# Recurrent channels laid out by heads: gathers replaced by operands in place, two vector steps moved to accumulating DMAs

## The chip, the cores and the metric

The kernel runs on one core of a Trainium2 chip. Its engines are TensorE (PE, matrix multiplications; the profile calls its weight loads PEld), VectorE (DVE), ScalarE (ACT), GpSimd (POOL) and SyncE (SP). Each engine works off its own list of instructions in order; SP and POOL issue the DMAs. The metric is the device time of one execution in microseconds (us). The time before is 1534.15 us, the median of three runs (1534.04 to 1534.54).

## The reference

One layer of a decoder trunk over 1024 positions with 1024 channels: a projection to 7168 channels, a convolution branch and a recurrent branch of 1536 channels in 16 heads of 96, both gated and merged, an output projection, and an MLP. What matters here is the projection and the recurrent branch:

```python
h = rms_norm(x, g_mix[l])
z = jnp.einsum("bsd,de->bse", h, w_in[l]) + b_in[l]
va, ga, xb, gb, sa, sb = jnp.split(z, cuts, axis=-1)

u = va * jax.nn.sigmoid(ga)
u = causal_depthwise_conv(u, conv_a_w[l], conv_a_b[l])      # 31 taps
u = jax.nn.silu(layer_norm(u, ln_g[l], ln_b[l]))
...
v = causal_depthwise_conv(xb, conv_b_w[l], conv_b_b[l])     # 4 taps
v = rg_lru(v, w_rg_a[l], b_rg_a[l], w_rg_x[l], b_rg_x[l], lam[l])
...
def rg_lru(x, w_a, b_a, w_x, b_x, lam):
    r = jax.nn.sigmoid(block_diag_linear(x, w_a, b_a))      # per head, 96x96
    i = jax.nn.sigmoid(block_diag_linear(x, w_x, b_x))
    log_a = -LRU_C * r * jax.nn.softplus(-lam)
    a = jnp.exp(log_a)
    bterm = jnp.sqrt(-jnp.expm1(2.0 * log_a)) * i * x
    ...                                                     # h = a*h + bterm along the positions
```

All inputs and outputs are float32. The kernel multiplies float32 in three passes: every operand is split in a high part (rounded to the format fp32r) and a low part (the rest), and high x high, low x high and high x low are summed in PSUM.

## The kernel before

Channels stand on the 128 partitions and the 1024 positions on the free axis. A tile `T` is 128x1024 float32 (512 KB); there are 37 buffers of that size, and a tile waits for the last reader of the buffer that it gets.

The projection's first part runs over 28 chunks of 128 output channels, in the order `CH`: value and gate chunks of the convolution branch (VA, GA) and the twelve chunks of the recurrent branch (XB). A chunk is 24 pairs of operands by two halves of 512 positions, 48 matmuls, on line 726. The first three chunks are done before the loop; the loop over slots `s` = 3 to 27 does one chunk in each slot and, beside it, the work of chunks and heads that came before. The order of every engine's instructions is written out by hand (`manual_schedule`): the Python code is the order. Only DVE's is planned: `later` puts work on a list with a time when its input should be ready, `vector_work` works off that list by these times, and `fill` puts taps of the 31-tap convolution (`conv`) in between as long as a running estimate of DVE's clock stays below the next ready time. The estimates are fixed numbers; nothing on the chip feeds back into them.

**A weight chunk** is loaded by SP (`w_load`, two slots ahead) and split by `split_dma` (lines 63 to 67): ACT writes l = -w, a POOL DMA adds w to it in place (an accumulating DMA), ACT writes h = w in fp32r. So l is the low part, rounded by h's conversion.

**A tile of v**: `xb_out` evacuates chunk XB+t in the slot behind it: ACT writes xb and the last tap of v, DVE adds the other three taps (`rest`, line 486). `xb_parts` (line 492) then splits v: ACT writes vth, DVE subtracts to get vtl (line 462 is the one place from which `dve` calls its functions, so many DVE instructions bear that line).

**A head** has 96 channels, so head n of group g (four heads in three tiles) lies in one or two tiles of v. `head_load` (line 505) gathers its 96 rows of vth and vtl from the tiles into vh and vl by SP DMAs, by the table `PIECES`. `head_w` loads the two 96x96 gate weights, `head_w_parts` splits them. `head_mm(n, gi)` does the six matmuls of gate gi (lines 534 to 536) into the tag "ps2", of which there is one PSUM buffer. `head_gate` writes the sigmoid on ACT (line 542) and scatters its rows back to the tiles `gate[gi, t]` by SP DMAs (line 549).

In slot `s`, with `before` the head whose first gate's matmuls ran in the slot before, and `new` the head of this slot, the order on PE is: 36 matmuls of the chunk, `head_mm(before, 1)`, 12 matmuls, `head_mm(new, 0)`. On ACT: gate 0 of `before`, the evacuation of the chunk before, the split of the next weights, `scan_root`, `xb_parts`, gate 1 of `before`, the split of the next head's weights, `scan_exp`.

**The scan** of group g: in the slot behind the group's last head (`EXP`), `scan_exp` computes a and a tanh on ACT (six instructions of 128x1024, lines 558 and 559, behind a load of ACT's table), and `scan_in` multiplies gate 1 with v on DVE for tiles 3g and 3g+1, a slot later for 3g+2. `scan_root` takes square roots a slot later, `scan_tile` runs the scan (lines 575 to 578) in the slots behind. Slots 9, 14, 19 and 24 are the EXP slots.

**The convolution** (`conv`) ends by writing its tile to DRAM (`yd`) and adding it to the tile `ysum` on DVE (line 651), for the mean of the layer norm. Four of the eight convolutions end in the slots of the projection's first part, the others in the next stage.

**The next stage** (z) does the remaining 28 chunks in pairs by a scheme of 7 products of half size. The weights of the products are sums of blocks (`z_sums`, names zs) on DVE, then split by `z_lhs` (names zo), mostly with `split_dma` again. The inputs' sums xs and their parts are made in slots 23 to 27 (`XS`, `x_load`, `x_sum`, `x_parts`).

Of the kernel before, what the change touches and what calls it, by code (L numbers as in the profile page):

```python
# [9 lines left out]
F32 = mybir.dt.float32  # L10
# [3 lines left out]
ALU = mybir.AluOpType  # L14
# [16 lines left out]
def trunk_kernel(ctx: ExitStack, tc: tile.TileContext, x, xt_in, xt_eo, vecs, w_in, w_a_out, w_b_pl, w_b_sq,  # L31
# [12 lines left out]
    def T(name, dt=F32, shape=(P, S)):  # L44
        return tp.tile(list(shape), dt, tag="T", name=name)
# [77 lines left out]
    def H(name, tag, dt=F32):  # L123
        return qp.tile([HD, S], dt, tag=tag, name=name, bufs=4 if tag == "p" else 2)
# [310 lines left out]
    def at(e, cost, ready=0.0):  # L435
        clk[e] = max(clk[e], ready) + cost
        return clk[e] + 0.1
# [3 lines left out]
    def fill(until):  # L441
        while clk["V"] + 0.67 <= until:
            if taps["now"] is None:
                if taps["next"] is None:
                    if not taps["wait"] or taps["hold"]:
                        return taps["more"](until)
                    taps["next"] = conv(taps["wait"].pop(0))
                    next(taps["next"])
                taps["now"], taps["next"], taps["left"] = taps["next"], None, 48
            if next(taps["now"], None) is None:  # L450
                taps["now"] = None
                continue
            taps["left"] -= 1
            if taps["left"] == 4 and taps["wait"] and not taps["hold"]:

                taps["next"] = conv(taps["wait"].pop(0))
                next(taps["next"])

    def dve(cost, ready, f, *a):
# [2 lines left out]
        f(*a)  # L462
        return at("V", cost, ready)


    PIECES = [[(0, 0, 96, 0)], [(0, 96, 128, 0), (1, 0, 64, 32)],
              [(1, 64, 128, 0), (2, 0, 32, 64)], [(2, 32, 128, 0)]]

    vt = {}

# [20 lines left out]

    def xb_parts(t):
        vp_[t] = T(f"vth{t}", F32R), T(f"vtl{t}", F32R)
        nc.scalar.activation(vp_[t][0], vt[t], AF.Copy)
        h = vp_[t][0].bitcast(F32)
        later(at("A", 1.06), 1.22, nc.vector.tensor_tensor, vp_[t][1], vt[t], h, ALU.subtract)


    gws = {}
# [2 lines left out]
    gate = {}  # L502
    hd = dp.tile([12, P, S], F32, name="hd")

    def head_load(n):

        g, hh = divmod(n, 4)
        parts[n] = H(f"vh{n}", "p", F32R), H(f"vl{n}", "p", F32R)
        for (ti, p0, p1, d0) in PIECES[hh]:
            for a, b in zip(parts[n], vp_[3 * g + ti]):  # L510
                nc.sync.dma_start(a[d0:d0 + p1 - p0, :].bitcast(F32), b[p0:p1, :].bitcast(F32))

    def head_w(n):
        raw = rp.tile([HD, 2, HD], F32, tag="rraw", name=f"rraw{n}")
# [11 lines left out]
    gps = {}  # L526

    def head_mm(n, gi):
        vh, vl = parts[n]
        gh, gl = gws[n]  # L530
        gps[n, gi] = ps = PS(f"rg{n}_{gi}", "ps2")
        for hf, hs in enumerate(HALVES):
            o = ps[:HD, hs]
            nc.tensor.matmul(o, gh[:, gi, :], vh[:, hs], start=True, stop=False)  # L534
            nc.tensor.matmul(o, gl[:, gi, :], vh[:, hs], start=False, stop=False)
            nc.tensor.matmul(o, gh[:, gi, :], vl[:, hs], start=False, stop=True)  # L536
        at("P", 6 * MM)

    def head_gate(n, gi, ready):
        g, hh = divmod(n, 4)  # L540
        a = H(f"g{n}_{gi}", "g")
        nc.scalar.activation(a, gps.pop((n, gi))[:HD, :], AF.Sigmoid,  # L542
                             bias=(ba_c, bx_c)[gi][:, n:n + 1])
        at("A", 1.11, ready)
        for (ti, p0, p1, d0) in PIECES[hh]:
            t = 3 * g + ti
            if (gi, t) not in gate:
                gate[gi, t] = T(f"g{gi}_{t}")
            nc.sync.dma_start(gate[gi, t][p0:p1, :], a[d0:d0 + p1 - p0, :])

    at_, rooted = {}, {}

# [49 lines left out]
    def conv(j):  # L602
        u = ut.pop(j)
        acc, tmp = T(f"y{j}"), T(f"yt{j}")
        xe, xo = (u[:, h] for h in HALVES)
        p0, p2 = (acc[:, h] for h in HALVES)
        xs, p1 = (tmp[:, h] for h in HALVES)
        bias = cab_c[:, j:j + 1]

        def tap(d):  # L610
            w = WA - 1 - d
            return caw[:, w * 8 + j:w * 8 + j + 1]

        def tapsum(k):

            return tap(2 * k) if k == NE - 1 else csum[:, NE - 2 - k, j:j + 1]

        sub, add = ALU.subtract, ALU.add
        nc.scalar.activation(p0, xe, AF.Identity, scale=tap(0), bias=bias)
        nc.scalar.activation(p1, xo, AF.Copy, scale=tap(1))  # L620
        begun = at("A", 1.24)
        yield True

        def step(cost=0.67):
            at("V", cost)
            return True

        nc.vector.tensor_tensor(xs, xe, xo, add)
        yield step()
        nc.vector.tensor_scalar(p2, xs, tapsum(0), cab2[:, j:j + 1], ALU.mult, add)  # L630
        clk["V"] = max(clk["V"], begun)
        yield step(0.45)
        for k in range(1, NE):
            for o, a, c in ((p0, xe, tap(2 * k)), (p2, xs, tapsum(k)),
                            (p1, xo, tap(2 * k + 1) if k < NE - 1 else None)):
                if c is not None:
                    nc.vector.scalar_tensor_tensor(o[:, k:], a[:, 0:HS - k], c, o[:, k:],  # L637
                                                   ALU.mult, add)
                    yield step()
        nc.vector.tensor_tensor(p2, p2, p0, sub)  # L640
        yield step()
        nc.vector.tensor_tensor(p2, p2, p1, sub)
        yield step()
        nc.vector.tensor_tensor(p0[:, 1:], p0[:, 1:], p1[:, 0:HS - 1], add)
        nc.sync.dma_start(yd[j], acc)
        yield step()
        if j == 0:
            ysum.append(T("ysum"))
            nc.vector.tensor_copy(ysum[0], acc)
        else:  # L650
            nc.vector.tensor_tensor(ysum[0], ysum[0], acc, add)
        yield step(1.22)

# [40 lines left out]
    def later(ready, cost, f, *a):  # L696

        todo.append((ready, len(todo), cost, f, a))
# [9 lines left out]
    def w_load(s):  # L708
        if s < NC1:
            wraw[s] = load_w(w_in[CH[s]], f"win{s}")  # L710
# [77 lines left out]
    def z_get(n, f):  # L788
# [1 line left out]

    ENGINES = {mybir.EngineType.Activation, mybir.EngineType.DVE, mybir.EngineType.PE,
               mybir.EngineType.SP, mybir.EngineType.Pool}
    HS0 = [5 + 5 * (n // 4) + n % 4 for n in range(NH)]
    head_at = {s: n for n, s in enumerate(HS0)}

    EXP = {head_slot: g for g, head_slot in enumerate(HS0[4 * g + 3] + 1 for g in range(4))}
    XS = {23: ((x_load, 0),), 24: ((x_sum, 0),), 25: ((x_load, 1), (x_parts, 0, 6)),
          26: ((x_sum, 1), (x_parts, 0, 7, 5)), 27: ((x_parts, 0, 4), (x_parts, 1, 6))}
    w_load(3)
    w_load(4)  # L800
    for c2 in range(4):
# [2 lines left out]
    with tc.manual_schedule(engines=ENGINES):  # L804
        for s in range(3, NC1):
            w_load(s + 2)
            taps["hold"] = s > NC1 - 4
            begun = clk["P"]
            clk["A"], clk["V"] = max(clk["A"], begun + 0.5), max(clk["V"], begun - 2)

            if s == 3:

                chunk_mm(s, 0, 24, (1,))
                rs = first_scale()
                first_product(0, rs)
                xb_out(0, zps[0])
                first_parts(rs)
                chunk_mm(s, 0, 24, (0,))
            else:
                chunk_mm(s, 0, 18)  # L820
            before, new, nxt = (head_at.get(s + d) for d in (-1, 0, 1))
            if before is not None:

                head_gate(before, 0, begun)
                head_mm(before, 1)
            if s > 3:
                chunk_mm(s, 18, 24)
            if new is not None:
                head_mm(new, 0)

# [3 lines left out]
            elif c >= GA:  # L834
                u_out(c - GA, zps[s - 2], zps[s - 1])
            w_parts(s + 1)
            if s - 1 in EXP:

                scan_root(EXP[s - 1])
            if s == 3 or c >= XB:  # L840
                vector_work(0)
                xb_parts(0 if s == 3 else c - XB)
            if before is not None:
                head_gate(before, 1, clk["P"] - 12 * MM)
            if nxt is not None:
                head_w_parts(nxt)
            if s == 5:
# [24 lines left out]
                for c2 in range(4):  # L872
                    nc.sync.dma_start(xu[0, c2], xc[c2])
            vector_work(clk["P"] - 0.7)
            if nxt is not None:
                head_load(nxt)

# [1272 lines left out]
def layout(i):  # L2152
# [13 lines left out]
    def tiles(w, n=1):  # L2166
# [4 lines left out]


    mix = np.arange(D).reshape(2, 4, 4, 32).transpose(0, 2, 1, 3).ravel()
    vecs = [cols(i[n][0]) for n in ("g_mix", "b_in")] + [cols(i["g_mlp"][0][mix])]
    vecs += [cols(i[n][0]) for n in ("conv_a_b", "ln_g", "ln_b")]
    vecs += [cols(i["conv_a_w"][0]), cols(i["conv_b_w"][0]), cols(i["conv_b_b"][0])]
    vecs += [cols(i["lam"][0])] + [heads(i[n][0]) for n in ("b_rg_a", "b_rg_x")]
    wb = i["w_b_out"][0].reshape(12, P, 8, P)
    w2 = i["w_2"][0].reshape(DFF // 512, 2, 2, P, 2, HS).transpose(0, 2, 4, 3, 1, 5)
    return {  # L2180
        "x": x,
# [2 lines left out]

        "xt_eo": x[:, mix].reshape(HS, 2, 4, 2, P).transpose(1, 2, 4, 3, 0).reshape(2, 4, P, S),
        "vecs": np.concatenate(vecs, 1),
        "w_in": tiles(i["w_in"][0]),
        "w_a_out": tiles(i["w_a_out"][0]),
        "w_b_pl": wb[[0, 1, 2, 3, 6, 7, 8, 9]].transpose(2, 1, 0, 3).reshape(8, P, S),
        "w_b_sq": wb[[4, 5, 10, 11]].reshape(2, 2, P, 4, 2, P).transpose(3, 2, 4, 0, 1, 5).reshape(4, P, S),  # L2190
# [34 lines left out]
```

## Time and profile before

| | before |
| --- | --- |
| median of the runs | 1534.15 us |
| the profiled execution's own time | 1534.4 us |
| its span, first to last instruction | 1532.6 us |
| PE busy | 99% of the span |
| DVE, ACT, POOL busy | 79%, 59%, 11% |
| DMA traffic | 304.68 MB, of it 24.4% of 16 engines' time by POOL's queue and 46.6% by SP's |

All times in the views are microseconds from the span's start. A row of a timeline is start, busy time, engine, line, operation, output<-inputs with their shapes, and in brackets the engine's idle time before it with what ended it. A row of the chain that ended last is start, time, engine, name and line; xN is the number of instructions in it. A row of waits is the waiting engine with its instruction, the releaser, and the total, the number and the longest of these waits. A row of DMA issues gives the number, the size of one and the median time from issue to landing. Line numbers are those of the kernel before.

### The profile page before, as it was taken

To read this page: it belongs to the slowest core of one execution; us is meant where nothing else is said; L and a number is where in the kernel's file an instruction comes from. 1 tells how busy PE (TensorE), PEld (TensorE's weight loads), DVE (VectorE), ACT (ScalarE), POOL (GpSimd) and SP (SyncE) were. 2 spreads that over 40 slices of the span, in tenths; PEclk is the share of its full clock that TensorE was granted. 3 is DMA by queue.
4 is the path that set the end of the run, shared out by engine and by line. 5 is a ranking of instruction groups with operands and counts; after the bars stand their busy time and mean duration, and the time that the engine had idled before them with its cause. 6 is when DMAs were issued, how large, how long until landed. Compare 5 with 4: busy or idle time off the path is not lost.

```text
span 1532.6 us, 19039 instructions
## 1 busy us (share of the span) xinstructions
PE 1522.9 (99%) x6734; PEld 1252.9 (82%) x6734; DVE 1217.2 (79%) x1647; ACT 911.8 (59%) x1273; POOL 172.6 (11%) x205
## 2 busy tenths in 40 slices
PE   9999999999999999999999999999999999999998
PEld 7878887888888888888888888888888888888886
DVE  6899999979999998778769879755555386777777
ACT  6648576657667666735475877554444455545475
POOL 0000000002222222000022322000000000101010
PEclk9999999999999999999999999999999999999999
DMA  8776978899998888963779898333333974776465
GB/s 349 198 188 159 250 185 215 223 274 224 241 255 209 198 193 229 311 230 117 265 199 301 197 194 210 138 117 112 112 112 110 304 266 124 177 209 170 109 123 153
DMA packets 132577, 304.68 MB, mean 199 GB/s; under 512 B 13264, under 2 KB 35280, under 8 KB 132480
## 3 DMA queue, kind: packets, MB, share of 16 engines
q1 hardware_dynamic: 104048, 234.79, 46.6%
q0 software_dynamic: 28288, 68.40, 24.4%
q8 instruction: 53, 0.87, 0.2%
q14 instruction: 44, 0.36, 0.1%
q10 hardware_dynamic: 144, 0.26, 0.0%
HBM read 149.79 MB, written 60.82 MB: 137 GB/s over the span
## 4 chain that ended last, share of the span: by engine, by line
PE 91%; issue 4%; DMA 2%; POOL 1%; DVE 1%; ACT 0%; SPq 0%; POOLq 0%; DVEq 0%
PE z L726 18%; PE d1b L1952 2%; PE d2b L1952 2%; PE d0b L1952 2%; PE d3b L1952 2%; PE d0e L1952 1%; PE d3e L1952 1%; PE d3a L1952 1%; PE d2e L1952 1%; PE d2a L1952 1%; PE d1e L1952 1%; PE d1a L1952 1%; PE z L258 1%; PE rg L534 1%; PE rg L536 1%
## 5 line engine op out<-in xcount | busy, mean ns | idle before, releaser
L726 PE MATMUL z<-xh,win_h 128*128 128x512 f32 x400 | 124.9, 390 | 0.0
L726 PE MATMUL z<-xl,win_h 128*128 128x512 f32 x400 | 124.5, 389 | 0.0
L726 PE MATMUL z<-xh,win_l 128*128 128x512 f32 x400 | 98.2, 391 | 0.0
L726 PEld LDWEIGHTS z<-xh,win_l 128*128 128x128 f32 x400 | 75.1, 188 | 16.9
L726 PEld LDWEIGHTS z<-xh,win_h 128*128 128x128 f32 x400 | 75.0, 188 | 16.7 <-ACT win_h L67 0.7
L637 DVE SCALAR_TENSOR_TENSOR y<-u,vec,y 128x511 f32<-128x511 f32 (+14 forms) x120 | 88.6, 739 | 0.0
L726 PEld LDWEIGHTS z<-xl,win_h 128*128 128x128 f32 x400 | 75.1, 188 | 15.8
L542 ACT ACTIVATE g<-rg,vec 96x1024 f32<-96x1024 f32 x32 | 35.6, 1113 | 85.4 <-issue 43.2
L637 DVE SCALAR_TENSOR_TENSOR yt<-u,vec,yt 128x511 f32<-128x511 f32 (+6 forms) x112 | 82.9, 740 | 0.0
L637 DVE SCALAR_TENSOR_TENSOR y<-yt,csum,y 128x511 f32<-128x511 f32 (+6 forms) x112 | 82.8, 739 | 0.0
L1648 ACT ACTIVATE o<-s 128x512 fp32r<-128x512 f32 x56 | 33.7, 623 | 45.7 <-DVE s L1632 26.4
L66 POOL DMA_DIRECT2D win_l<-win_raw x25 | 21.8, 871 | 325.0 <-ACT win_l L65 287.5
L486 DVE SCALAR_TENSOR_TENSOR v<-xb,vec,v 128x1023 f32<-128x1023 f32 (+2 forms) x36 | 46.2, 1283 | 6.9 <-ACT v L477 6.1
L66 POOL DMA_DIRECT2D zo<-zw x42 | 36.7, 874 | 127.7 <-ACT zo L65 114.6
L66 POOL DMA_DIRECT2D db_10l<-br x4 | 3.5, 874 | 339.3 <-DMA br<-in_w_dram 253.8
L1176 DVE TENSOR_TENSOR o<-s,o 128x512 fp32r<-128x512 f32 x56 | 37.3, 684 | 1.5 <-ACT o L1648 1.5
L65 ACT ACTIVATE zo<-zw 128x512 fp32r<-128x512 f32 x42 | 26.3, 625 | 20.1 <-PE z10f L914 2.1
L66 POOL DMA_DIRECT2D zo<-zs x28 | 24.5, 875 | 76.7 <-ACT zo L65 71.4
L578 DVE TENSOR_TENSOR_SCAN g<-a,g 128x1024 f32<-128x1024 f32 x12 | 27.5, 2292 | 0.4
L67 ACT ACTIVATE win_h<-win_raw 128x1024 fp32r<-128x1024 f32 x25 | 26.1, 1046 | 0.0
L65 ACT ACTIVATE win_l<-win_raw 128x1024 fp32r<-128x1024 f32 x25 | 26.1, 1045 | 0.0
L67 ACT ACTIVATE zo<-zw 128x512 fp32r<-128x512 f32 x42 | 26.1, 621 | 0.0
(3140 smaller groups left out, 4832.2 us busy)
## 6 DMA issues: line engine op xcount, KB each, us to landing
w_raw<-in_w_dram SPq DMA_DIRECT2D x34, 512.0 KB, 5.6
br<-in_w_dram SPq DMA_DIRECT2D x32, 512.0 KB, 5.9
ar<-fd SPq DMA_DIRECT2D x32, 512.0 KB, 6.8
zw<-in_w_in_dram SPq DMA_DIRECT2D x28, 512.0 KB, 5.7
win_raw<-in_w_in_dram SPq DMA_DIRECT2D x25, 512.0 KB, 7.4
win_l<-win_raw POOLq DMA_DIRECT2D x25, 512.0 KB, 7.3
zo<-zw POOLq DMA_DIRECT2D x42, 256.0 KB, 5.7
gates<-zg SPq DMA_DIRECT2D x32, 256.0 KB, 3.9
```

Source lines behind the costliest of these rows:

```text
L65: nc.scalar.activation(l, src, AF.Copy, scale=-1.0)
L66: nc.gpsimd.dma_start(l, src, accum_op=ALU.add)
L67: nc.scalar.activation(h, src, AF.Copy)
L258: nc.tensor.matmul(z0[i][:, HALVES[hf]], w0[i][w][:, k, :], xpart(a, hf, k), start=k == 0 and which == "hh", stop=k == 7 and which == ("hl ...
L486: nc.vector.scalar_tensor_tensor(v[:, d:S], a[:, 0:S - d], cbw_c[:, w * 12 + t:w * 12 + t + 1], v[:, d:S], ALU.mult, ALU.add)
L542: nc.scalar.activation(a, gps.pop((n, gi))[:HD, :], AF.Sigmoid, bias=(ba_c, bx_c)[gi][:, n:n + 1])
L578: nc.vector.tensor_tensor_scan(i, a, i, 0.0, ALU.mult, ALU.add)
L637: nc.vector.scalar_tensor_tensor(o[:, k:], a[:, 0:HS - k], c, o[:, k:], ALU.mult, add)
L726: nc.tensor.matmul(zps[s][:, HALVES[hf]], w[:, k, :], xw[k][part][hf], start=n == 0, stop=n == 23)
L1176: tt(l, src, h.bitcast(F32), ALU.subtract)
L1648: nc.scalar.activation(o[:, 0], src, AF.Copy)
L1952: nc.tensor.matmul(o, a, b, start=start and n == 0, stop=stop and n == len(todo) - 1, skip_group_check=not start or not stop)
```

## The change

The recurrent branch's 1536 channels are put in another order on the host: of each group of 384 channels, tile i holds the 96 channels of head i in rows 0 to 95, and 32 channels of the fourth head in rows 96 to 127. The columns of `w_in` and `b_in` for xb and gb, the convolution's weights, `lam` and the rows of `w_b_out` are permuted with it; the gate weights and their biases by heads stay.

With that, heads 0 to 2 of a group use rows 0 to 95 of the tiles vth and vtl directly, and their gates are written by ACT straight into the tile `gate[gi, t]`. Only head 3 is put together from three pieces of 32 rows by SP (`head_load`, now called for a tile at the start of the slot behind its split), and its gates are scattered in three pieces of 32 rows. 24 pieces of vh and vl (before 48) and 24 pieces of gates (before 48) are left.

Two DVE steps go to POOL's DMA queue: the low halves vtl (by `split_dma`, so ACT copies v twice) and the sum `ysum`.

The order changes too: heads begin one slot sooner (slots 4 to 7, 9 to 12 and so on), so the EXP slots are 8, 13, 18 and 23; the split of v moves from the end of its slot to the middle of the slot behind; the chunk's matmuls are cut at 24 of 48 and no longer at 36; and gate 1 stands ahead of `scan_root` on ACT and no longer behind it and the split of v. The convolution's counter of instructions left goes from 48 to 47, and the DVE work of a slot is handed out once a slot.

```diff
@@ fill
-                taps["now"], taps["next"], taps["left"] = taps["next"], None, 48
+                taps["now"], taps["next"], taps["left"] = taps["next"], None, 47
...
-    PIECES = [[(0, 0, 96, 0)], [(0, 96, 128, 0), (1, 0, 64, 32)],
-              [(1, 64, 128, 0), (2, 0, 32, 64)], [(2, 32, 128, 0)]]
...
     def xb_parts(t):
         vp_[t] = T(f"vth{t}", F32R), T(f"vtl{t}", F32R)
-        nc.scalar.activation(vp_[t][0], vt[t], AF.Copy)
-        h = vp_[t][0].bitcast(F32)
-        later(at("A", 1.06), 1.22, nc.vector.tensor_tensor, vp_[t][1], vt[t], h, ALU.subtract)
+        split_dma(vt[t], *vp_[t])
+        parts[4 * (t // 3) + t % 3] = vp_[t]
+        at("A", 2.1)
...
-    def head_load(n):
-
-        g, hh = divmod(n, 4)
-        parts[n] = H(f"vh{n}", "p", F32R), H(f"vl{n}", "p", F32R)
-        for (ti, p0, p1, d0) in PIECES[hh]:
-            for a, b in zip(parts[n], vp_[3 * g + ti]):
-                nc.sync.dma_start(a[d0:d0 + p1 - p0, :].bitcast(F32), b[p0:p1, :].bitcast(F32))
+    def head_load(t):
+
+        n = 4 * (t // 3) + 3
+        if t % 3 == 0:
+            parts[n] = H(f"vh{n}", "p", F32R), H(f"vl{n}", "p", F32R)
+        for a, b in zip(parts[n], vp_[t]):
+            nc.sync.dma_start(a[32 * (t % 3):32 * (t % 3) + 32, :].bitcast(F32), b[HD:P, :].bitcast(F32))
+        del vp_[t]
...
     def head_gate(n, gi, ready):
         g, hh = divmod(n, 4)
-        a = H(f"g{n}_{gi}", "g")
+        if hh < 3:
+            gate[gi, 3 * g + hh] = T(f"g{gi}_{3 * g + hh}")
+        a = gate[gi, 3 * g + hh][:HD] if hh < 3 else H(f"g{n}_{gi}", "g")
         nc.scalar.activation(a, gps.pop((n, gi))[:HD, :], AF.Sigmoid,
                              bias=(ba_c, bx_c)[gi][:, n:n + 1])
         at("A", 1.11, ready)
-        for (ti, p0, p1, d0) in PIECES[hh]:
-            t = 3 * g + ti
-            if (gi, t) not in gate:
-                gate[gi, t] = T(f"g{gi}_{t}")
-            nc.sync.dma_start(gate[gi, t][p0:p1, :], a[d0:d0 + p1 - p0, :])
+        if hh == 3:
+            for i in range(3):
+                nc.sync.dma_start(gate[gi, 3 * g + i][HD:P, :], a[32 * i:32 * i + 32, :])
...
@@ conv
         nc.sync.dma_start(yd[j], acc)
-        yield step()
         if j == 0:
             ysum.append(T("ysum"))
-            nc.vector.tensor_copy(ysum[0], acc)
+            nc.gpsimd.dma_start(ysum[0], acc)
         else:
-            nc.vector.tensor_tensor(ysum[0], ysum[0], acc, add)
-        yield step(1.22)
+            nc.gpsimd.dma_start(ysum[0], acc, accum_op=add)
+        yield step()
...
-    HS0 = [5 + 5 * (n // 4) + n % 4 for n in range(NH)]
+    HS0 = [4 + 5 * (n // 4) + n % 4 for n in range(NH)]
...
@@ the loop over slots
             w_load(s + 2)
+            for t in sorted(vp_):
+                head_load(t)
...
-                chunk_mm(s, 0, 18)
+                chunk_mm(s, 0, 12)
             before, new, nxt = (head_at.get(s + d) for d in (-1, 0, 1))
             if before is not None:
 
                 head_gate(before, 0, begun)
                 head_mm(before, 1)
+            if made:
+                xb_parts(made.pop())
             if s > 3:
-                chunk_mm(s, 18, 24)
+                chunk_mm(s, 12, 24)
...
             w_parts(s + 1)
+            if before is not None:
+                head_gate(before, 1, clk["P"] - 30 * MM)
             if s - 1 in EXP:
 
                 scan_root(EXP[s - 1])
             if s == 3 or c >= XB:
-                vector_work(0)
-                xb_parts(0 if s == 3 else c - XB)
-            if before is not None:
-                head_gate(before, 1, clk["P"] - 12 * MM)
+                made.append(0 if s == 3 else c - XB)
...
             vector_work(clk["P"] - 0.7)
-            if nxt is not None:
-                head_load(nxt)
...
@@ on the host
+    r = np.arange(NH * HD).reshape(NH // 4, 4, HD)
+    rnn = np.concatenate([r[:, :3], r[:, 3].reshape(NH // 4, 3, 32)], 2).ravel()
+    z = np.arange(7168)
+    for o in (2048, 3584):
+        z[o:o + NH * HD] = o + rnn
```

In slots 8, 13, 18 and 23 of the kernel after, DVE's order is: the two products of `scan_in` for tiles 3g and 3g+1, then the three taps of `rest` for the tile of v that was evacuated in this slot, then the split of the next head's weights and taps of the convolution. In the EXP slots of the kernel before, the order of these was `rest`, then the products.

More of the change, by code (lines that the diff above doesn't have):

```diff
@@ L528, in head_mm @@
     def head_mm(n, gi):
-        vh, vl = parts[n]
+        vh, vl = (a[:HD] for a in (parts.pop(n) if gi else parts[n]))
         gh, gl = gws[n]
@@ L798, in trunk_kernel @@
           26: ((x_sum, 1), (x_parts, 0, 7, 5)), 27: ((x_parts, 0, 4), (x_parts, 1, 6))}
+    made = []
+    head_w(0)
     w_load(3)
@@ L2173, in layout @@
     mix = np.arange(D).reshape(2, 4, 4, 32).transpose(0, 2, 1, 3).ravel()
-    vecs = [cols(i[n][0]) for n in ("g_mix", "b_in")] + [cols(i["g_mlp"][0][mix])]
+    r = np.arange(NH * HD).reshape(NH // 4, 4, HD)
[3 more added lines that the diff above has]
+        z[o:o + NH * HD] = o + rnn
+    vecs = [cols(i["g_mix"][0]), cols(i["b_in"][0][z])] + [cols(i["g_mlp"][0][mix])]
     vecs += [cols(i[n][0]) for n in ("conv_a_b", "ln_g", "ln_b")]
-    vecs += [cols(i["conv_a_w"][0]), cols(i["conv_b_w"][0]), cols(i["conv_b_b"][0])]
-    vecs += [cols(i["lam"][0])] + [heads(i[n][0]) for n in ("b_rg_a", "b_rg_x")]
-    wb = i["w_b_out"][0].reshape(12, P, 8, P)
+    vecs += [cols(i["conv_a_w"][0]), cols(i["conv_b_w"][0][:, rnn]), cols(i["conv_b_b"][0][rnn])]
+    vecs += [cols(i["lam"][0][rnn])] + [heads(i[n][0]) for n in ("b_rg_a", "b_rg_x")]
+    wb = i["w_b_out"][0][rnn].reshape(12, P, 8, P)
     w2 = i["w_2"][0].reshape(DFF // 512, 2, 2, P, 2, HS).transpose(0, 2, 4, 3, 1, 5)
@@ L2186, in layout @@
         "vecs": np.concatenate(vecs, 1),
-        "w_in": tiles(i["w_in"][0]),
+        "w_in": tiles(i["w_in"][0][:, z]),
         "w_a_out": tiles(i["w_a_out"][0]),
```

## The prediction

> **What bounds the kernel now.** I read the page first, then the stretches with each engine's busy time, then the chain of waits, then the timelines of single slots. The page and the stretches of the projection part (first time us: end, then busy time of each engine):
>
> ```profile
> PE 1522.9 (99%) x6734; PEld 1252.9 (82%) x6734; DVE 1217.2 (79%) x1647; ACT 911.8 (59%) x1273; POOL 172.6 (11%) x205
> 50.00:110.00 60.00, 59.97 (x264) 48.29 (x263) 56.66 (x98) 32.05 (x35) 4.75 (x6) 1.00 0.77 192
> 110.00:175.00 65.00, 65.00 (x286) 51.99 (x285) 61.59 (x77) 42.97 (x45) 3.92 (x5) 1.00 0.79 198
> 175.00:245.00 70.00, 70.00 (x308) 56.24 (x307) 66.73 (x77) 48.02 (x50) 5.26 (x6) 1.00 0.84 214
> 245.00:330.00 85.00, 85.00 (x373) 68.14 (x372) 72.70 (x86) 51.16 (x53) 5.23 (x6) 1.00 0.83 223
> ...
> 361.10 2.72 PE z0a L914 x12
> ```
>
> PE works all the time: 264+286+308+373 = 1231 matmuls in 280 us are 227.5 ns each, and the best stretch, the last row (from the chain that ended last), has 2.72/12 = 226.7 ns. All that a smoother order could win here is 1231 x 0.0008 = 1.0 us. DVE is busy 92%, yet PE doesn't wait for it. So the change can hide, or add waits.
>
> One group of four heads has five slots of PE work. Of the slot that runs exp and tanh ("exp slot", 118.58 to 130.93), here are PE's chain, then ACT, DVE and POOL:
>
> ```profile
> 118.58 8.18 PE z L726 x36
> 126.76 0.23 PE rg L534
> ...
> 128.16 13.65 PE z L726 x60
> 143.20 8.28 PE z L726 x36
> ...
> 118.62 1.11 ACT L542 ACTIVATE g<-rg,vec 96x1024 f32<-96x1024 f32 x1 [2.15 <-PE rg L536]
> 122.87 1.04 ACT L67 ACTIVATE win_h<-win_raw 128x1024 fp32r<-128x1024 f32 x1
> 128.35 1.06 ACT L494 ACTIVATE vth<-v 128x1024 fp32r<-128x1024 f32 x1 [4.44 <-issue]
> 129.32 1.09 ACT L542 ACTIVATE g<-rg,vec 96x1024 f32<-96x1024 f32 x1
> 138.68 1.10 ACT L474 ACTIVATE xb<-z,vec 128x1024 f32<-128x1024 f32 x1
> 147.13 1.04 ACT L494 ACTIVATE vth<-v 128x1024 fp32r<-128x1024 f32 x1
> 148.07 0.35 ACT L522 ACTIVATE rgh<-rraw 96x192 fp32r<-96x192 f32 x1
> 149.74 1.12 ACT L542 ACTIVATE g<-rg,vec 96x1024 f32<-96x1024 f32 x1
> ...
> 124.35 3.92 DVE L486 SCALAR_TENSOR_TENSOR v<-xb,vec,v 128x1023 f32<-128x1023 f32 x3
> 128.19 2.35 DVE L462 TENSOR_TENSOR g<-g,v 128x1024 f32<-128x1024 f32 x2
> 130.46 1.22 DVE L462 TENSOR_TENSOR vtl<-v,vth 128x1024 fp32r<-128x1024 f32 x1
> 131.87 0.74 DVE L637 SCALAR_TENSOR_TENSOR yt<-u,vec,yt 128x508 f32<-128x508 f32 x1
> 132.52 0.74 DVE L637 SCALAR_TENSOR_TENSOR y<-u,vec,y 128x507 f32<-128x507 f32 x1
> ...
> 123.26 0.87 POOL L66 DMA_DIRECT2D win_l<-win_raw  x1 [12.83 <-DMA g<-g]
> ```
>
> A chunk of 48 matmuls is 48 x 0.2267 = 10.88 us, six head matmuls (126.76 to 128.16, between the first two rows) 1.39; a tap is 0.655 us from start to start, v's three taps (v L486) 3.84 and the two products of the scan's input (g<-g,v) 2.27.
>
> **The change, part by part.** *Removed from DVE:* 12 low halves vtl and 8 steps of ysum, 20 x 1.22 = 24.4 us. PE waited for none of it, so it is worth 0 to the 1.0 us above; I take 0. *SP:* the gathers of v (vh, vl) and most scatters of gates become operands in place; only head 3 of a group still moves, in pieces of 32 rows. I take 0 for the smaller traffic. *ACT:* each tile of v gets one more copy, 12 x 1.0 us; ACT is idle 22 of 65 us in the second stretch (42.97 busy). Cost 0, if its place holds (below). *POOL:* 20 DMAs of 0.87 us each, for an engine that mostly idles:
>
> ```profile
> POOL win_l L66 <- ACT win_l L65: 287.5, 22, 37.4
> ...
> win_l<-win_raw POOLq DMA_DIRECT2D x25, 512.0 KB, 7.3
> yd<-y SPq DMA_DIRECT2D x8, 512.0 KB, 5.9
> ...
> g<-g SPq DMA_DIRECT2D x16, 128.0 KB, 5.1
> ...
> win_l<-win_raw POOLq DMA_DIRECT2D x1, 512.0 KB, 4.5
> ...
> g<-g SPq DMA_DIRECT2D x1, 128.0 KB, 3.2
> ...
> DMA to landing us min/median/max: 4.5/7.0/10.3
> ...
> DMA to landing us min/median/max: 2.4/4.2/14.3
> ```
>
> The last two rows are of L66 in the projection part (the accumulating 512 KB DMA, the same kind that vtl now uses) and of L549 (the gates' scatters); the rows with x1 are of the window 116 to 131, with a weight load in flight; those with x25, x8 and x16 of the page's list. A ysum DMA waits for a conv's end, and the weight's split stands behind it in POOL's order; the split is issued 123.26-118.58 = 4.7 us into a slot, lands 7.0 later and is read 2/3 into the next (12.35+8.2), some 8 us spare. Cost 0.
>
> *The wait that is added.* In the exp slot DVE's order is now: products for tiles 3g and 3g+1, then v's three taps of the next group's first tile. Before, these products needed gates of heads 0 to 2, long landed. Now every tile has 32 rows of head 3, whose second gate is computed in this very slot. From the slot's start t: 24 matmuls and 6 head matmuls end at 5.44+1.39 = 6.83; gate 1 on ACT (moved up, behind win_h, which ends 122.87+1.04-118.58 = 5.33) ends at 8.0; SP issues the scatter at 8.06; it lands Lg later. Then DVE does 2.27 and v's 3.84: v is ready at X = 8.06+Lg+2.27+3.84 = 14.2+Lg. With 3.2 us, X = 17.4. Behind the waiting product stand v's taps and all conv taps; for v waits ACT (copy -v), for that the accumulating DMA, for that PE's head.
>
> ACT, in order: gate 1, rgh, exp and tanh take from 129.32 to 138.68, 9.4 us; gate 1 starts at 6.9, so ACT is free at 16.3 and X is 1.1 us past it. From X: two copies of v 1.9, then the work from 138.68 to 150.86 less the copy that is gone (147.13 to 148.07): gate 0 of the next group's first head ends at X+13.1. Behind it two copies 1.9, xb and v 2.3, the split 2.0, gate 1 1.0: X+20.3. PE needs that gate's PSUM buffer (there is one) at 12.35+10.88+1.39+12.28 = 36.9 (exp slot, next slot with its head, then two half chunks and head matmuls). So PE stands for X-16.6 = 0.8 us a group. The landing L of vtl binds instead if X+1.25+L is past 23.7 (third matmul of that head), so L over 5.8 adds L-5.8. The first group with this wait has little else in flight (a 512 KB split in the window 116 to 131 landed in the 4.5 of the row): 0.8. In the next two, ysum and yd move 1 MB more; I take L between 4.5 and 7.0 but nearer the median, 6.5: 0.8+0.7 = 1.5 each. Sum 3.8. Bounds per group: Lg 2.4 and L under 5.8, 0; both medians (4.2, 7.0), 1.8+1.2 = 3.0.
>
> The Trainium skill, "DMA: Bandwidth & Descriptors", section "Anatomy of one DMA — SWDGE (gpsimd) path", fits 2.0 us plus bytes/436e3 to a DMA issued from GpSimd, an estimate of 3.2 us for 512 KB. The 25 rows of L66 never came under 4.5, so the trace disagrees; by the page no landing would bind and the three groups would cost 0.8 each, 2.4 in all.
>
> *After the last exp slot* no head follows, but DVE is late, and the next stage's first weight sums stand behind it:
>
> ```profile
> L578 DVE TENSOR_TENSOR_SCAN g<-a,g 128x1024 f32<-128x1024 f32 x12 | 27.5, 2292 | 0.4
> ...
> 321.74 1.23 DVE L462 TENSOR_TENSOR xs<-xs,xs 128x1024 f32<-128x1024 f32 x1 [8.36 <-DMA xs<-xu]
> ...
> 360.99 0.69 DVE L462 TENSOR_TENSOR zs<-zw,zw 128x512 f32<-128x512 f32 x1
> ...
> 363.36 0.87 POOL L66 DMA_DIRECT2D zo<-zs  x1 [2.32 <-ACT zo L65]
> ...
> 372.44 2.71 PE z0b L914 x11
> ...
> PEld z0b L914 <- DMA zo<-zs: 0.3, 1, 0.3
> ...
> DMA to landing us min/median/max: 4.0/6.5/9.4
> ```
>
> Before, zs starts 0.1 us ahead of the stage (361.10), its split is issued 2.4 later, and PE waits 0.3 us for it: no slack. After, from the product at t+11.3 (8.06+3.2) DVE has to do, by start-to-start times, a pass over 1024 columns at 1.13 to 1.22: 3 products 3.4, 8 differences xs 9.8 (their loads are issued right behind the scatter and land while DVE works), two scan tiles 9.7 (each the scan of 2.29 and two passes with gaps), two u 2.4, three xsl 3.4, and 31 taps with a conv's two first steps 21.4: 50.1 us, so zs starts at t+61.4. PE starts the stage at t+12.35+4x10.88 = t+55.9. That is 5.5 us into the stage, its split issued at 7.9, landed at the median of L66 in 359 to 400 (last row) at 14.4; PE wants the low half at 372.44+0.45-361.10 = 11.8. Stall 2.6; with 4.0 it is 0.1, with 9.4 and a later scatter (4.2) 6.5. Before, DVE idled 8.36 us at the xs loads in this stretch; that this idle goes is what keeps the lateness at 5.5 us. Should the loads be late again, it is 8 us more.
>
> *Sum* on the profiled execution's own 1534.4: +3.8+2.6 = 1540.8; the median lies 0.25 lower, so 1540.5 us.
>
> **Rivals.**
>
> *Hidden.* The scatter lands in its minimum, 2.4: X = 16.6 and PE waits 0 in all three groups; the sums come at 4.7, the split lands in 4.0, PE waits nothing; up to 1.0 us of smoother PE. Time 1533.2 to 1534.2, and with half of the forecast's waits 1537. For it: the quiet scatters, and less traffic by SP, so shorter landings than the rows say. Against: a weight load and an accumulating DMA are in flight at just this point, and the 128 KB scatters have a median of 5.1 on the page's list. It stops holding once Lg passes 2.4. That the freed 24.4 us of DVE make it faster would need over 3.07 us, three times what PE can win.
>
> *The landings decide.* Both medians, 4.2 and 7.0: 3 x 3.0 = 9.0 in the groups and, sums 1.0 later, 3.6 at the stage's start: 1534.4+12.6-0.25 = 1546.8. For it: 4.2 and 7.0 are medians over just such slots. Against: these medians come from a kernel that has twice as many transfers on SP.
>
> **How the numbers follow.** What a measurement can't tell from no change is 0.2%, 3.07 us: 1531.1 to 1537.2. Forecast, PE held up by the late product: 0.5. Landings: 0.16. Hidden and half hidden: 0.30. Faster by a way that I don't see: 0.04. Of the forecast's half, about 0.06 falls under 1537.2 (the group's wait at 0 to 0.3 each, the start's at 2.6). So slower 0.6, same 0.36, faster 0.04. Range 1533.4 to 1548.0, from the hidden case's times to the landings' with a little over; the likeliest alone has 1537 to 1545.
>
> **What would show it.** In each exp slot a DVE idle of some 8 us before g<-g,v, ended by DMA g<-g (step 1); ACT idle before the copy -v, ended by DVE v, of 1 us (step 2); PE or PEld waits in the slots behind at rg, by ACT g or by DMA vtl, 0.8 to 1.5 us each, none for the last group (step 3); zs about 5.5 us behind the stage's first matmul and z0b waiting 2 to 4 us for DMA zo<-zs (step 4). It would be wrong if these products do not wait or PE shows no new wait in the group, or if PE waits for a weight's low half behind a ysum DMA on POOL, which I cost at 0.

## The result, and the profile after

The changed kernel takes 1550.03 us (median; 1549.65 to 1551.99), the kernel before 1534.35 (1534.04 to 1534.79): ratio 1.0105, 95% interval 1.0093 to 1.0117. It is 15.7 us slower, where 6.4 us slower was forecast, with a range up to 1548.0. The way it goes was right, the size was not.

The stretches of the projection part and of the next stage's start after the change, and last the same stretch of that start before it (first time us: end, then the busy time of each engine with its instructions, the granted PE clock, the DMA share and GB/s):

```profile
110.00:175.00 65.00, 64.99 (x286) 51.84 (x284) 56.36 (x68) 46.85 (x49) 6.90 (x8) 1.00 0.69 166
175.00:245.00 70.00, 68.08 (x296) 53.90 (x295) 63.30 (x79) 49.41 (x51) 7.85 (x9) 1.00 0.71 164
245.00:330.00 85.00, 82.42 (x354) 65.88 (x353) 69.77 (x89) 58.61 (x60) 9.88 (x11) 0.98 0.74 173
361.00:400.00 39.00, 32.60 (x135) 25.83 (x134) 38.76 (x53) 22.79 (x35) 7.87 (x9) 0.96 0.80 199
...
361.00:400.00 39.00, 39.00 (x173) 32.04 (x172) 34.95 (x49) 27.88 (x45) 7.37 (x10) 1.00 0.86 213
```

PE's count of matmuls tells where the time went. In the same stretches the kernel before did 286, 308, 373 and 173. So 0, 12, 19 and 38 matmuls are missing, which at 0.2275 us are 0, 2.7, 4.3 and 8.6 us: 15.6 in all. The first group lost nothing that shows, the second and third lost 7.0, and the start of the next stage lost the most. The traffic fell as it should (0.83 to 0.74 of the DMA engines' time from 245 to 330), and DVE has less to do; neither bought anything.

The rows of waits, first two of the whole kernel, then PE's own from 40 to 420 us (engine, line, releaser: total, number, longest):

```profile
DVE g L462 <- DMA g<-g: 28.5, 4, 8.2
ACT vtl L65 <- DVE v L483: 15.9, 7, 4.0
...
PE rg L534 <- DMA vtl<-v: 4.0, 2, 2.6
PE z0a L914 <- ACT z0b L952: 3.7, 1, 3.7
PE z1a L914 <- DMA zo<-zw: 1.7, 1, 1.7
PE z0a L914 <- DMA zo<-zw: 1.0, 1, 1.0
```

The first row is the wait that was forecast: DVE's product of the scan's input waits once in each of the four exp slots for the scatter of the fourth head's second gate. The second is ACT waiting for v: three of its seven waits, 6.7 us, stand behind these products (below), the others in other slots. The third is PE waiting for v's low half. The timelines of ACT and DVE in the exp slots of the three groups that matter:

```profile
114.61 1.11 ACT L542 ACTIVATE g<-rg,vec 96x1024 f32<-96x1024 f32 x1 [1.56 <-PE rg L534]
124.25 1.06 ACT L65 ACTIVATE vtl<-v 128x1024 fp32r<-128x1024 f32 x1 [0.17 <-DVE v L483]
180.67 1.11 ACT L542 ACTIVATE g<-rg,vec 96x1024 f32<-96x1024 f32 x1 [1.56 <-PE rg L534]
192.68 1.06 ACT L65 ACTIVATE vtl<-v 128x1024 fp32r<-128x1024 f32 x1 [2.54 <-DVE v L483]
249.10 1.11 ACT L542 ACTIVATE g<-rg,vec 96x1024 f32<-96x1024 f32 x1 [1.57 <-PE rg L534]
262.57 1.06 ACT L65 ACTIVATE vtl<-v 128x1024 fp32r<-128x1024 f32 x1 [4.00 <-DVE v L483]
...
118.02 2.36 DVE L462 TENSOR_TENSOR g<-g,v 128x1024 f32<-128x1024 f32 x2 [8.18 <-DMA g<-g]
186.45 2.36 DVE L462 TENSOR_TENSOR g<-g,v 128x1024 f32<-128x1024 f32 x2 [5.97 <-DMA g<-g]
256.34 2.36 DVE L462 TENSOR_TENSOR g<-g,v 128x1024 f32<-128x1024 f32 x2 [7.44 <-DMA g<-g]
258.62 3.92 DVE L483 SCALAR_TENSOR_TENSOR v<-xb,vec,v 128x1023 f32<-128x1023 f32 x3
```

The first ACT row of each pair is the second gate; it starts some 7 us into the slot (7.05 from the slot's first matmul, where 6.9 was worked out). From it to ACT's copy of v pass 9.6, 12.0 and 13.5 us: ACT itself waits 0.17, 2.54 and 4.00 us. What differs is the scatter. Here are the DMA issues of the windows around the three gates, in that order, and between them the sums' DMAs of the second and third group (size of one, median us to landing):

```profile
g<-g SPq DMA_DIRECT2D x3, 128.0 KB, 2.3
...
ysum<-y POOLq DMA_DIRECT2D x1, 512.0 KB, 6.9
...
g<-g SPq DMA_DIRECT2D x3, 128.0 KB, 4.6
...
ysum<-y POOLq DMA_DIRECT2D x1, 512.0 KB, 8.0
...
g<-g SPq DMA_DIRECT2D x3, 128.0 KB, 6.1
...
DMA to landing us min/median/max: 4.5/4.6/5.8
```

2.3 us in the first group, 4.6 and 6.1 in the others, where a convolution has just ended and its sum is in flight on POOL's queue (issued at 179.0 and 247.7; the convolution's store yd is issued behind the scatter, at 185.8 and 255.3). The prediction's X = 14.2+Lg gives 16.5, 18.8 and 20.3 us into the slot, and the copies start at 16.7, 19.1 and 20.5. The last row, of POOL's twelve vtl DMAs, says that v's low half always lands in 4.5 to 5.8 us. The forecast put the convolution's traffic on that landing; it fell on the scatter.

The Trainium skill, "DMA: Bandwidth & Descriptors", section "Issuing engines are not separate DMA queues", says that DMAs of different issuing engines run on the same 16 DMA engines and interleave; these rows agree, with a 128 KB scatter of SP at 2.3 us without POOL's sum and 6.1 us beside it.

The start of the next stage, in order SP, DVE, ACT and the chain that ended last, and behind these the chain's row of the same product before the change:

```profile
325.90 0.60 SPq L60 DMA_DIRECT2D win_raw<-in_w_in_dram  x1
347.60 0.32 SPq L577 DMA_DIRECT2D hd<-g  x1
350.94 2.79 SPq L737 DMA_DIRECT2D zw<-in_w_in_dram  x4
...
345.28 2.29 DVE L576 TENSOR_TENSOR_SCAN g<-a,g 128x1024 f32<-128x1024 f32 x1
377.13 0.70 DVE L462 TENSOR_TENSOR zs<-zw,zw 128x512 f32<-128x512 f32 x1
...
378.59 0.63 ACT L65 ACTIVATE zo<-zs 128x512 fp32r<-128x512 f32 x1 [2.26 <-DVE zs L462]
380.59 0.58 ACT L952 ACTIVATE z0b<-z0a 128x512 f32<-128x512 f32 x1
...
381.22 4.46 PE z0a L914 x12
...
367.00 2.72 PE z0a L914 x12
```

The stage's first matmul starts at 368.18, and zs comes 9.0 us later (before: together with it). ACT, in order, waits for zs to split it, and behind that split stands the copy z0b, for which PE's third product z0a waits: from zs to that product 381.22-377.13 = 4.1 us. Two more things can be read: SP issued nothing for 21 us, because the store of a scan tile (hd) stands in its queue and that tile came late from DVE; and the third product is slow, 4.46 us for 12 matmuls where the same one took 2.72 before.

The windows right behind PE's two longest stops (length, PE's busy time with its matmuls, granted clock, DMA share, GB/s) show why:

```profile
268.80:273.00 4.20, 4.20 (x13) 0.63 0.66 125
381.30:385.70 4.40, 4.40 (x13) 0.64 0.55 129
```

Behind the longest wait of each place (2.6 us by the row of vtl, 3.7 by that of z0b) PE is busy without a gap, but 13 matmuls take 4.2 to 4.4 us: the clock is granted at 0.63 on the average of the window, and within it at 0.50 from 269.9 to 273.3 us and from 382.5 to 385.9. That is 4.2-13x0.2275 = 1.2 us and 1.4 us more in these windows alone. Stops of 1.0, 1.4 and 1.7 us show no such tail.

### The profile page after: what moved, and what is told of

The parts are those of the page before. It is cut to its first block, busy times and chain, and to the rows that moved or that the text cites. A ratio compares the mean times of both kernels' runs of the same rounds, so it can differ in the third digit from the quotient of the medians.

```text
span 1548.3 us, 18952 instructions
## 1 busy us (share of the span) xinstructions
PE 1527.9 (99%) x6734; PEld 1254.8 (81%) x6734; DVE 1194.2 (77%) x1627; ACT 924.3 (60%) x1286; POOL 189.7 (12%) x225
## 4 chain that ended last, share of the span: by engine, by line
PE 71%; DVE 3%; issue 2%; DMA 1%; POOL 1%; SPq 0%; ACT 0%; POOLq 0%; DVEq 0%
PE d0b L1952 2%; PE d2b L1952 2%; PE d1b L1952 2%; PE d3b L1952 2%; PE d0e L1952 1%; PE d3e L1952 1%; PE d3a L1952 1%; PE d2e L1952 1%; PE d2a L1952 1%; PE d1a L1952 1%; PE d0a L1952 1%; PE d1e L1952 1%; PE yb3b L1086 1%; PE yb2b L1086 1%; PE yb1b L1086 1%
## 5 line engine op out<-in xcount | busy, mean ns | idle before, releaser
L723 PE MATMUL z<-xh,win_l 128*128 128x512 f32 x400 | 95.0, 389 | 0.0
L65 ACT ACTIVATE zo<-zw 128x512 fp32r<-128x512 f32 x42 | 26.4, 627 | 32.6 <-DMA zw<-in_w_in_dram 10.2
L462 DVE TENSOR_TENSOR g<-g,v 128x1024 f32<-128x1024 f32 x12 | 14.3, 1221 | 28.5 <-DMA g<-g 28.5
L462 DVE TENSOR_TENSOR zo<-zs,zo 128x512 fp32r<-128x512 f32 x28 | 19.3, 688 | 15.6 <-ACT zo L764 15.6
```

Source lines behind the costliest of these rows:

```text
L65: nc.scalar.activation(l, src, AF.Copy, scale=-1.0)
L723: nc.tensor.matmul(zps[s][:, HALVES[hf]], w[:, k, :], xw[k][part][hf], start=n == 0, stop=n == 23)
```

## The experiments

The ratio behind each time is against the kernel before on the same chip.

**The products behind v's taps** (product_late):

```diff
-                        scan_in(begun + 3.5, 3 * g, 3 * g + 1)
+                        scan_in(begun + 12.0, 3 * g, 3 * g + 1)
```

> Edit: the planner's ready time of the two products in an exp slot goes from 3.5 to 12.0 us behind the slot's start, so that v's three taps and some conv taps stand ahead of them. Theory (the product that waits for the fourth head's second gate holds up v, and with it DVE, SP's queue behind the scan's store, and the next stage's weights): the stalls of PE in the groups (0.3, 2.5 and 4.7 us) and most of the 8.8 us at the next stage's start go, 1534 to 1537 us. Rival (the start of the next stage is late for a reason of its own, the loads behind the scan's store on SP): only the groups' 7.5 us go, 1542 to 1543. Rival (the accumulating DMA of v's low half is too slow): the groups' stalls stay, 1548 to 1550.

1539.18 us, ratio 1.0031 (1.0019 to 1.0042). The groups lose nothing any more: no wait of PE at rg is left. 5.0 us are left at the next stage's start, more than the theory said and less than either rival. Its wait of PE and its zs:

```profile
PE z0a L914 <- ACT z0b L952: 3.3, 1, 3.3
...
366.11 0.68 DVE L462 TENSOR_TENSOR zs<-zw,zw 128x512 f32<-128x512 f32 x1
```

The stage starts at 360.8 here, so zs is 5.3 us late without any product ahead of v: a second cause. Behind the wait of 3.3 us the clock is granted at 0.50 from 369.3 to 376.2 us, so a good part of what is left is the slow clock: PE does 145 matmuls from 361 to 400, 28 fewer than before, which is 6.4 us. (This profile is of the slowest of the run's seven executions, 1540.38.)

**The norm's sum on DVE again** (ysum_on_dve):

```diff
-                taps["now"], taps["next"], taps["left"] = taps["next"], None, 47
+                taps["now"], taps["next"], taps["left"] = taps["next"], None, 48
...
+        yield step()
         if j == 0:
             ysum.append(T("ysum"))
-            nc.gpsimd.dma_start(ysum[0], acc)
+            nc.vector.tensor_copy(ysum[0], acc)
         else:
-            nc.gpsimd.dma_start(ysum[0], acc, accum_op=add)
-        yield step()
+            nc.vector.tensor_tensor(ysum[0], ysum[0], acc, add)
+        yield step(1.22)
```

> Edit: the sum of the norm is added on DVE again, as before the change. Theory (the accumulating DMA of ysum is in flight together with the scatter of the second gate in exp slots 13, 18 and 23 and doubles its landing, 2.25 us without it against 4.6 and 6.1): the scatters land in 2.3 us in all groups, v is ready 16.5 us into the exp slot, PE loses 0 to 0.5 us a group, 6.5 to 7 us less in all; the next stage starts with DVE some 2 us less late: 1540 to 1543. Rival (the landing varies with other traffic, not with ysum): 1549 to 1551, scatters at 4 to 6 us still.

1542.57 us, ratio 1.0053 (1.0038 to 1.0068). The scatters of the second and third group (windows 180 to 184 and 247 to 251), PE's only wait for a low half, and four rows of PE at the next stage's start:

```profile
g<-g SPq DMA_DIRECT2D x3, 128.0 KB, 2.3
...
g<-g SPq DMA_DIRECT2D x3, 128.0 KB, 2.3
...
PE rg L534 <- DMA vtl<-v: 0.5, 1, 0.5
...
368.75 0.74 PE L915 MATMUL z1a<-xh,zo 128*128 128x512 f32 x2 [2.73 <-DMA zo<-zw]
369.56 0.63 PE L915 MATMUL z1a<-xh,zo 128*128 128x512 f32 x2
374.31 0.62 PE L915 MATMUL z0a<-xh,zo 128*128 128x512 f32 x1 [2.73 <-ACT z0b L953]
375.16 1.06 PE L915 MATMUL z0a<-xh,zo 128*128 128x512 f32 x2
```

Both land as in the first group, and 4.0 us of waiting become 0.5. That the accumulating DMA of the sum was what doubled the scatter is shown, most cleanly in the second group: there the convolution still ends just ahead of the scatter (the sum on DVE at 178.7), while in the third it ends behind it (258.5). Of the 24 us taken off DVE, the 10 us of the sum cost 7.5 us as DMAs (1550.03-1542.57). Nearly all that is left stands at the next stage's start, 140 matmuls from 361 to 400 where the kernel before did 173. The four rows are of two equal stops there: behind the first the matmuls go on at the full rate, behind the second at half of it.

**The weight blocks loaded a slot sooner** (zload_early):

```diff
-            if s == NC1 - 3:
+            if s == NC1 - 4:
                 for i in range(4):
                     z_load(i // 2, i % 2)
```

> Edit: the four loads of the next stage's first weight blocks (zw) are issued one slot sooner, so on SP ahead of the store of the first scan tile of the last group and of the loads xs. Theory (SP, in order, stood from 326 to 347 us behind that store, which waits for the late DVE; then 13 transfers bunch up and the zw blocks take 11 to 17 us): the waits of the stage's first two products for DMA zo<-zw go (1.1 and 1.9 us), the copy z0b comes sooner, but the sums zs on DVE are still 9 us late: 8.8 us shrink to some 4, 1545 to 1546. If the late DVE alone made the start late: 1549 to 1550. If SP's order made all of it: 1541.

1550.89 us, ratio 1.0108 (1.0093 to 1.0124): no gain. That is nearest to the second of the three outcomes (0.9 us above it), not to mine. The waits for zo<-zw are gone, and the next one has taken all of it:

```profile
PE z0a L914 <- ACT z0b L952: 6.8, 1, 6.8
...
377.34 0.69 DVE L462 TENSOR_TENSOR zs<-zw,zw 128x512 f32<-128x512 f32 x1
```

zs is where it was (377.13). SP's 21 us behind the store were real, yet not on the path: DVE's own lateness sets the start.

**v's low half on DVE again** (vlow_on_dve):

```diff
-        split_dma(vt[t], *vp_[t])
+        nc.scalar.activation(vp_[t][0], vt[t], AF.Copy)
+        h = vp_[t][0].bitcast(F32)
+        dve(1.22, at("A", 1.06), nc.vector.tensor_tensor, vp_[t][1], vt[t], h, ALU.subtract)
         parts[4 * (t // 3) + t % 3] = vp_[t]
-        at("A", 2.1)
```

> Edit: v's low half is subtracted on DVE again, at the new place in the order. Theory (v itself is late, and behind it ACT's chain of two gates through the single PSUM buffer, X-16.6): PE no longer waits for the landing of vtl, but for the gates that come 2.2 and 3.6 us late in the second and third group; the groups lose 5 to 7 us still, 1548 to 1551. Rival (the landing of 4.5 us is what PE waits for): the stalls of 1.6 and 2.8 us with the half clock behind the second go, 1543 to 1545.

1547.81 us, ratio 1.0089 (1.0074 to 1.0104), 2.2 us below the changed kernel, just under what the theory allowed. PE's waits in the groups are now for DVE, and they stand in the first and second group; the third loses nothing (374 matmuls from 245 to 330):

```profile
PE rg L535 <- DVE vtl L462: 4.4, 2, 2.8
...
194.64 1.06 ACT L491 ACTIVATE vth<-v 128x1024 fp32r<-128x1024 f32 x1 [2.76 <-DVE v L483]
200.74 1.22 DVE L462 TENSOR_TENSOR vtl<-v,vth 128x1024 fp32r<-128x1024 f32 x1
```

The subtraction is 5 us behind its input, since DVE works off conv taps that the planner put ahead for a clock on which DVE is not late. In the third group the convolution's sum is issued at 266.3, long behind the scatter, so that scatter has no sum beside it. So this run doesn't isolate the landing of 4.5 us cleanly; it shows that DVE is no quicker place for the step as long as it is late.

**Late products and no new convolution** (late_hold), and **with the early loads** (late_hold_zload): product_late with

```diff
-            taps["hold"] = s > NC1 - 4
+            taps["hold"] = s > NC1 - 7
```

> Edit: the products late as in product_late, and no new convolution is begun from slot 22 to the next stage (before the change none was begun there either), so that 31 taps no longer stand ahead of the sums zs on DVE. Theory (what product_late still loses, 4.9 us, is ACT waiting for a late zs with the copy z0b behind it, and zs is late by those taps): zs comes some 3 us into the stage, set by ACT's xs6h behind the weight loads, and PE loses 0 to 0.7 us: 1534 to 1535.5. Rival (the loads zw that land late set zs, taps or not): 1538 to 1539.5 as product_late.

> Edit: late_hold, and the loads zw a slot sooner as in zload_early. Theory: with DVE in time, ACT no longer waits for zw and zs comes before 2 us into the stage: no loss left at the stage's start, 1533.5 to 1534.5, no more than 1 us below the kernel before, since PE has no more to win. Rival (the freed 24 us of DVE are worth something once nothing is late): 1530 to 1533.

1534.71 us, ratio 1.0001 (0.9993 to 1.001), and 1534.17 us, ratio 0.9998 (0.9989 to 1.0006): both as expected. Of late_hold, the wait of DVE, zs, and PE's chain:

```profile
DVE g L462 <- DMA g<-g: 10.3, 3, 8.0
...
361.26 0.68 DVE L462 TENSOR_TENSOR zs<-zw,zw 128x512 f32<-128x512 f32 x1
...
361.42 2.72 PE z0a L914 x12
```

zs comes with the stage's start again, and PE waits for nothing. The two edits take back all of the 15.7 us, so the two causes, the early products and the 31 taps ahead of zs, are the whole loss. One product still waits 8.0 us, in the last exp slot, and there it costs nothing. Neither version is faster than the kernel before: the rival that the freed DVE time has a worth is out (1530 to 1533 expected by it).

**Only the second edit** (hold_only; the line above alone):

> Edit: only the second part of late_hold: no new convolution from slot 22; the products stay early. Theory (the late DVE holds SP at the store of a scan tile, and with it the zw loads): 8 to 12 taps less ahead of that store let SP go on some 8 us sooner; the groups' 7.5 us stay, of the 8.8 us at the next stage 1 to 3 are left: 1542 to 1545. If the waiting products alone made DVE late and the taps cost nothing: 1549 to 1551.

1542.65 us, ratio 1.0057 (1.0042 to 1.0072). The groups' waits stay and the stage's start is nearly free:

```profile
PE rg L534 <- DMA vtl<-v: 3.7, 2, 2.6
...
PE z0a L914 <- ACT z0b L952: 0.3, 1, 0.3
```

Against the kernel before in the same round of runs (1534.48 and 1534.21), 8.2 us here are the groups' share (with some 1 us at the stage's start), 5.0 in product_late the taps' share. They add to 13.2; the other 2.5 us come only with both. DVE is then late for both reasons; how much of the 2.5 is the slow clock, which falls differently in each run, stays open.

**Heads one slot later again** (heads_later):

```diff
-    HS0 = [4 + 5 * (n // 4) + n % 4 for n in range(NH)]
+    HS0 = [5 + 5 * (n // 4) + n % 4 for n in range(NH)]
```

> Edit: heads begin in slot 5 again as before the change (exp slots 9, 14, 19, 24), the rest stays. Theory (v is late only against heads that begin one slot sooner; v is now wanted 13 us later): DVE still waits 6 to 8 us for the scatter in each exp slot, but the groups lose nothing; DVE is late by 4 to 5 us at the next stage's sums, 2.5 to 3.5 us there: 1536.5 to 1538.5. Rival (the wait of DVE costs by itself, wherever v is wanted): 1541 to 1550.

1545.24 us, ratio 1.0073 (1.006 to 1.0087): a miss, the rival's outcome. PE's largest waits for 40 to 420 us and ACT's copy in the third group:

```profile
PE z L723 <- ACT win_h L67: 5.5, 2, 4.1
...
277.37 1.06 ACT L65 ACTIVATE vtl<-v 128x1024 fp32r<-128x1024 f32 x1 [5.23 <-DVE v L483]
282.50 1.04 ACT L67 ACTIVATE win_h<-win_raw 128x1024 fp32r<-128x1024 f32 x1
```

No head wants v yet, but ACT stands 5.2 us at its copy all the same, and behind the copy stands the split of the next weight chunk. I had counted when v is wanted and not what is queued behind the instruction that waits for it.

## Why the prediction was right or wrong

**Removed DVE and SP work: worth 0 to 1.0 us.** Right, shown by late_hold and late_hold_zload: all of the change's relief, and the same time. Nor did PE wait for a weight's low half behind a ysum DMA, which the prediction put at 0.

**The wait that is added.** The chain was right: the product waits for the scatter in each exp slot, X = 14.2+Lg holds within 0.3 us, and PE's loss in the groups comes near X-16.6 (-0.1, 2.2 and 3.7; read from the missing matmuls 0, 2.7 and 4.3). PE stands through most of it at the landing of vtl, 1.4 and 2.6 us, where X+1.25+4.6-23.7 gives 1.0 and 2.5; at the gate's one PSUM buffer it waits 0.5 in all, in the second group. product_late removed it whole. The size was off by one term: "lands Lg later", 3.2 us for all groups. It measured 2.3, 4.6 and 6.1. The prediction had the cause on the page, "ysum and yd move 1 MB more", and put it on "L between 4.5 and 7.0", the landing of vtl, which measured 4.5 to 5.8. The sum's DMA is issued 1.4 to 1.7 us ahead of the second gate, so it meets the scatter and not the split some 15 us later. The groups cost 7.0 and not 3.8. The groups would have cost 2.4 by the estimate that the prediction works out from the Trainium skill ("DMA: Bandwidth & Descriptors", section "Anatomy of one DMA — SWDGE (gpsimd) path"); the vtl landings stayed above its 3.2 us here too.

**After the last exp slot.** The step "PE wants the low half at ... 11.8. Stall 2.6" failed: the low half of zo made from zs was not what PE met first, and PE's rows show no wait for it. ACT's split of zs stands ahead of the copy z0b, and the third product needs that copy 367.00-361.10 = 5.9 us into the stage. By that path zs at 5.5 us would already have cost 5.5+4.1-5.9 = 3.7. And zs came at 9.0: the scatter 1.5 us later than taken (4.7 in this slot), 1.4 at the xs loads, and 0.6 that I can't place over 50 us of work. 9.0+4.1-5.9 = 7.2, with the slow clock of 1.4 behind it 8.6, what the missing matmuls say. What was right is that DVE's backlog sets it: zload_early shows that nothing else did, and hold_only that leaving out the 31 taps ahead of zs is enough to bring the start's loss down to some 1 us.

**A term that wasn't there.** The sum was short by 9.3 us. The clock behind a long stop is 1.4 of them at the stage's start. In the third group the slow matmuls cost 1.2 us or more, but PE no longer waits at the PSUM buffer there, so no more than 4.3-3.7 = 0.6 of that comes on top.

**Rivals.** "The landings decide" gave 1546.8 with scatters at 4.2 and vtl at 7.0: the right place for the first, the wrong one for the second. "Hidden" needed scatters at 2.4; only the first group had that.

## What to carry to other kernels

Where an engine works off a list in order, a new wait is priced by what is queued behind the waiting instruction on that engine and on the next ones down, and not by when its own result is wanted: the copy of v cost PE even where no head wanted v. When work is moved to a DMA, ask which other transfer is in flight at the moment it is issued, and look for a small one that somebody waits for. A hand-made plan that places filler work by fixed estimates turns one unforeseen wait into lateness everywhere after it; a later ready time for the one instruction (here 12.0 in place of 3.5 us) repaired the groups, and leaving filler work out ahead of the next stage repaired the rest.

## What the runs showed of the hardware

In the changed kernel, PE's stops with waits of 2.6 and 3.7 us were followed by 3.4 us at half the clock (granted 0.50), those of 1.0, 1.4 and 1.7 us by none. The length of the stop does not decide it alone: in ysum_on_dve two stops of 2.73 us each stand at 368.75 and 374.31, and only the second has the half rate behind it (0.43 us from matmul to matmul, against 0.23). What decides between them no run here shows. The Trainium skill, "TensorE: Matmul & The Clock Gate", section "What's actually happening", gives half the rate after an idle window of about 3.4 us; the half rate agrees, while the stop in the third group, with its wait of 2.6 us, was shorter than that window and set it off all the same.

A 128 KB scatter of SP landed in 2.3 us without the sum's 512 KB accumulating DMA, and in 4.6 and 6.1 us beside it. A weight split's DMA of the same kind, issued 0.5 us ahead of the sum's in these two places, does not do it by itself: in ysum_on_dve it is issued at 178.5 and lands 4.5 us later, and the scatter of the second group takes 2.3.
